# The opening transfers of a one-core hybrid encoder step: reordered, cut finer, spread over two queues

## The chip, the core and the metric

The kernel runs on one core of a Trainium2 chip. The metric is the device time of one execution in microseconds (us), median of several runs. The engines are named as in the profile: PE is TensorE (matrix products; PEld its weight loads), DVE is VectorE, ACT is ScalarE, POOL is GpSimd, SP is SyncE, which issues most transfers.

## What is computed

One inference step of a two-layer encoder over 288 rows (256 of a prompt, 32 of a running stream) of width 2048, in float32. Layer 0 mixes tokens by a gated MLP, layer 1 by retention; each is followed by a SwiGLU feed-forward part and each residual by a layer norm:

```
x = layer_norm(ALPHA * x + mixer(x), ...)
x = layer_norm(ALPHA * x + swiglu(x, w_ffn_in[i], w_ffn_out[i]), ...)
# the first mixer begins with the product that this change feeds:
z = gelu(x @ w_in)              # w_in: 2048 x 4096
u, v = split(z, 2);  v = layer_norm(v)
```

## The kernel before, in words

All weights lie in one packed array, cut into chunks of 512 KB: 128 partitions by eight blocks of 128x128. The blocks are packed in the order in which PE uses them. Float32 products are made of two halves: `split` (L591) casts a raw chunk on ACT to its high part (`whi`, L592) and subtracts on DVE to get the low part (`wlo`, L593). The same is done with each tile of x (`xh`, `xl`; loaded raw into `y`). For each block, `step` (L106) issues three products in this order: high by high (L112), high weights by low x (L113), low weights by high x (L114). PE runs in the order of the program; `prep` (L69) is called when a chunk's first block comes up and prepares three chunks ahead.

The first product group (`core.group("a_in", ...)`, L728) takes eight column tiles at once, so that chunk c, for c from 0 to 15, holds the eight blocks that meet x tile c. A chunk of the group therefore needs the x tile of its number too. Raw chunks go through a ring of three buffers (`raw`), the halves through rings of four (`whi`, `wlo`). SP's queue issues the transfers in the order of the program's schedule; a transfer into a ring buffer waits until the DVE subtraction that last read it is done. ACT, DVE and SP run their own instructions strictly in the order given.

At the start (L1114 to L1130) ACT loads its table, PE runs eleven warming products of a constant tile (L1117), and chunks 0 to 3 and x tiles 0 to 3 are prepared by hand order on ACT and DVE. Chunk 0 comes in two halves, chunk 1 whole, x in pairs of tiles. Further x tiles follow by `load` (L1120) from the group's hook, and after some steps `tables` (L627) brings the mask and mixing weights that DVE multiplies (`g_ws`, L633) and ACT casts (`g_w`, L638).

Of the kernel before, what the change touches and what calls it, by code (L numbers as in the profile page):

```python
# [10 lines left out]
F32 = mybir.dt.float32  # L11
# [8 lines left out]
P = 128  # L20
D = 2048
KT = D // P
NP = 256
NS = 32
NT = NP + NS
NH = NT // 2
ROW = 320
# [11 lines left out]
CB = 8  # L39
# [11 lines left out]
class Core:  # L51


    def __init__(self, ctx, tc, wpack):
        self.tc, self.nc, self.wpack = tc, tc.nc, wpack
        self.order = []
        self.wp = ctx.enter_context(tc.tile_pool(name="wp", bufs=4))
        self.wp.tile([P, 16], F32, tag="shift", name="shift_wp", bufs=1)
        self.acc = ctx.enter_context(tc.tile_pool(name="acc", bufs=4, space=PSUM))
        self.aux = ctx.enter_context(tc.tile_pool(name="aux", bufs=4, space=PSUM))  # L60
        self.dram = ctx.enter_context(tc.tile_pool(name="dram", bufs=1, space=bass.MemoryType.DRAM))
        self.ready = {}
        self.keep = {}
        self.nprep = 0
        self.todo = []
        self.soon = []
        self.ticks = 0

    def prep(self, upto, between=None):  # L69
        nc = self.nc  # L70
        while self.nprep <= upto and self.nprep < NCH:
            c = self.nprep
            raw = self.wp.tile([P, CB * P], F32, tag="raw", name=f"raw{c}", bufs=3)
            hi = self.keep[c] if c in self.keep else self.wp.tile([P, CB * P], F32R, tag="whi", name=f"whi{c}")
            lo = self.wp.tile([P, CB * P], F32R, tag="wlo", name=f"wlo{c}")
            n = CB * P
            dma, cut = {0: (n // 2, n // 4), 1: (n, n // 2)}.get(c, (n, n))
            for o in range(0, n, cut):
                if o % dma == 0:
                    nc.sync.dma_start(raw[:, o:o + dma], self.wpack[c][:, o:o + dma])  # L80
                q = slice(o, o + cut)
                split(nc, hi[:, q], lo[:, q], raw[:, q])
                if between is not None and o == 0:
                    between()
            self.ready[c] = (hi, lo)
            self.nprep += 1

# [497 lines left out]
def moving(pool, n, name, tag=None, lead=False):  # L585

    t = pool.tile([P, n, ROW], F32R, name=name, **({"tag": tag} if tag else {}))
    return t if lead else t[:, :, LEAD:]


def split(nc, hi, lo, f, pin=lambda i: i):  # L591
    pin(nc.scalar.copy(hi, f))  # L592
    nc.vector.tensor_tensor(lo, f, hi.bitcast(F32), ALU.subtract)  # L593


def to_rows(nc, room, src, w, prompt, sample):


    blocks = room.rearrange("(b s) f -> s b f", s=32)
    for a in range(4):  # L600
        nc.gpsimd.dma_start(blocks[:, :, a * w:(a + 1) * w], src[32 * a:32 * a + 32, :, :])
    nc.gpsimd.dma_start(prompt, room[:NP, :].rearrange("(t p) f -> p t f", p=P))
    nc.gpsimd.dma_start(sample, room[NP:, :])


def gmlp(core, cst, x, y, lnp, ins, v_out, load):
    tc, nc = core.tc, core.nc
    xh, xl = x
    xs = lambda k: (xh[:, k, :NT], xl[:, k, :NT])
    with ExitStack() as es:  # L610
        pool = es.enter_context(tc.tile_pool(name="gm", bufs=1, reuse_waits="tile"))
        sh = moving(pool, KT, "g_sh")
        tv = pool.tile([P, KT * ROW], F32, tag="sl", name="g_tv")
        tv = tv[:, :KT * NT].rearrange("p (q b i s) -> p q b i s", q=4, b=9, i=4)
        vp = pool.tile([P, 2, D], F32, name="g_vp")
        vs = y.rearrange("p k n -> p (k n)")[:NS, :D]
        v3 = pool.tile([NR, D], F32R, name="g_v3")
# [17 lines left out]
        def sample_weights():  # L635
# [2 lines left out]
                nc.scalar.copy(w3[r * NS:(r + 1) * NS], w)  # L638
            nc.vector.tensor_tensor(w3[2 * NS:], w, w3[:NS].bitcast(F32), ALU.subtract)

        nc.gpsimd.memset(nrm[:, 2, 0:2], 1.0)
        core.after(6, tables)
        core.after(12, sample_weights)
# [2 lines left out]
        def v_evac(m, ps):  # L646
            j = m - 16
            vg = pool.tile([P, NT], F32, tag="u", name=f"vg{j}", bufs=8)
            nc.scalar.activation(vg, ps[:, :NT], AF.Gelu)
            q, i = divmod(j, 4)  # L650
            nc.vector.transpose(tv[:, q, :, i, :], vg)
            if i == 3:
                t = tv[:, q, :, :, :].rearrange("p b i s -> p b (i s)")
                cs = slice(q * 512, (q + 1) * 512)
                to_rows(nc, core.room([NT, 512], f"g_room{q}"), t, P, vp[:, :, cs], vs[:NS, cs])
                core.after(2, lambda: v_rows(q))

        def v_rows(q):
            for t in range(3):
                n = rows[t]  # L660
                tc.keep_in_program_order(nc.vector.bn_stats(st[:n, t, q, :], vt[t][:n, q * 512:(q + 1) * 512]))
            if q == 3:
                v_stats()
# [62 lines left out]
        late = {}  # L726
        gbs = {}
        core.group("a_in", 0, list(range(KT)), list(range(16, 24)), xs, v_evac, load, lag=0)  # L728
        core.tiles("a_in", 0, list(range(KT)), list(range(24, 32)), xs, v_evac, grouped=False)
        core.tiles("a_in", 0, list(range(KT)), list(range(16)), xs, u_evac, grouped=False)  # L730
        ln = PostNorm(core, cst, x, y, lnp, 0)
# [361 lines left out]
@with_exitstack  # L1093
def hybrid_step(ctx, tc, ins, outs):
    nc = tc.nc
    ctx.enter_context(tc.manual_schedule(engines={PE}))
    core = Core(ctx, tc, ins["wpack"])
    cp = ctx.enter_context(tc.tile_pool(name="cp", bufs=1))
    lnp = ctx.enter_context(tc.tile_pool(name="lnp", bufs=1))
    cp.tile([P, 72], F32, name="shift")  # L1100
    lnp.tile([P, 32], F32, name="shift_lnp")
    core.wide_x = moving(cp, KT, "xh", lead=True)
    xh = core.wide_x[:, :, LEAD:]
    core.wide_l = moving(cp, KT, "xl", lead=True)
    xl = core.wide_l[:, :, LEAD:]
    y = cp.tile([P, KT, NT], F32, name="y")
    cst = {}
    cp.tile([P, 40], F32, name="shift_one")
    cst["one2048"] = cp.tile([P, P], F32, name="one2048")
    nc.gpsimd.memset(cst["one2048"], 1.0 / D)  # L1110
    cst["ln"] = cp.tile([P, 4, 2, KT], F32, name="lnv")
    cst["one_r"] = cp.tile([P, P], F32R, name="one_r")
    cp.tile([P, 56], F32, name="shift_end")
    core.tables("gelu_and_others")  # L1114
    nc.scalar.copy(cst["one_r"], cst["one2048"])
    warm = core.bank("warm")
    for _ in range(11):  # L1117
        nc.tensor.matmul(warm[:, :P], cst["one2048"], cst["one2048"], start=True, stop=True)

    def load(k):  # L1120
        if k < KT:
            if k % 2 == 0:
                nc.sync.dma_start(y[:, k:k + 2, :], ins["xT"][:, k:k + 2, :])
            split(nc, xh[:, k, :NT], xl[:, k, :NT], y[:, k, :])

    with tc.manual_schedule(engines={mybir.EngineType.DVE, mybir.EngineType.Activation}):
        core.prep(0, lambda: load(0))
        for k in range(1, 4):
            load(k)
            core.prep(k)  # L1130
    x = (xh, xl)
    ln = gmlp(core, cst, x, y, lnp, ins, outs["v"], lambda s: load(s + 4))
    ln = ffn(core, cst, x, y, lnp, 0, ln)
    ln = retention(core, cst, x, y, lnp, ln, ins, outs["st_p"], outs["st_s"])
    ffn(core, cst, x, y, lnp, 1, ln, outs["yT"], ins["gb_rows"])
    core.flush()
    assert len(core.order) == NBLK + NSTATE
    return core.order
# [85 lines left out]
```

## Time and profile before

| | |
|---|---|
| time, median of 3 runs | 2770.11 us (2769.72 to 2770.37) |
| the profiled execution's own time | 2770.98 us |
| its span, first to last instruction | 2769.2 us |
| PE busy | 2762.4 us |
| DVE busy | 1699.9 us |
| ACT busy | 1258.9 us |
| moved by DMA | 515.53 MB, mean 186 GB/s |

The page gives busy times of the engines, a strip of the span in 40 slices, and the chain of work that ended last. The first slice is 69 us long, so what this change touches has to be read from narrower views: rows of the timeline (start, duration, engine, line, operation, output from inputs, and in brackets the idle time before it with what ended it), and windows (for each engine busy time and a count of instructions; then the granted PE clock, the busy share of the DMA engines and GB/s).

### The profile page before, as it was taken

How to read it: one execution, taken by the hardware profiler on the slowest of the kernel's cores; microseconds unless marked ns; L12 is line 12 of the kernel's file. 1: busy time of each engine (PE TensorE's matmuls, PEld its weight loads, DVE VectorE, ACT ScalarE, POOL GpSimd, SP SyncE). 2: the span in 40 equal slices, each digit the busy share in tenths (PEclk: the TensorE clock that was granted, in tenths of full speed). 3: DMA queues.
4: the chain of work that ended last, by engine and by line, in shares of the span. 5: the costliest groups of instructions: out<-in, count | busy, mean ns of one | idle time of the engine just before them, and what ended most of it. 6: DMA issues, size and time to landing. Idle time of an engine off the chain costs nothing.

```text
span 2769.2 us, 51638 instructions
## 1 busy us (share of the span) xinstructions
PE 2762.4 (100%) x21618; PEld 2752.1 (99%) x21618; DVE 1699.9 (61%) x2493; ACT 1258.9 (45%) x1701; POOL 144.7 (5%) x245
## 2 busy tenths in 40 slices
PE   9999999999999999999999999999999999999999
PEld 9999999999999999999999999999999999999999
DVE  6688964445444456877765666767854445444466
ACT  5455554433344344644543444455643433444444
POOL 1100000000000000012200111210000000000001
PEclk9999999999999999999999999999999999999999
DMA  8655555555555555567765666765555555555554
GB/s 278 213 188 168 168 175 175 173 172 173 176 174 172 173 176 182 169 213 233 238 204 176 195 218 213 224 207 173 171 172 175 175 172 173 174 175 173 172 174 141
DMA packets 146794, 515.53 MB, mean 186 GB/s; under 512 B 18096, under 2 KB 20800, under 8 KB 146528
## 3 DMA queue, kind: packets, MB, share of 16 engines
q1 hardware_dynamic: 132272, 473.62, 51.6%
q0 software_dynamic: 14288, 38.60, 4.7%
q8 instruction: 169, 2.77, 0.4%
q14 instruction: 65, 0.53, 0.1%
HBM read 486.99 MB, written 25.17 MB: 185 GB/s over the span
## 4 chain that ended last, share of the span: by engine, by line
PE 98%; DMA 1%; DVE 1%; issue 0%; POOL 0%; ACT 0%; SPq 0%; POOLq 0%; DVEq 0%; ACTq 0%
PE af_in L112 13%; PE af_in L114 13%; PE af_in L113 13%; PE ab_in L112 7%; PE ab_in L114 7%; PE ab_in L113 7%; PE af_out L113 6%; PE af_out L112 6%; PE af_out L114 6%; PE ab_out L114 2%; PE ab_out L112 2%; PE ab_out L113 2%; PE aa_in L114 2%; PE aa_in L113 2%; PE aa_in L112 2%; PE aa_out L112 1%
## 5 line engine op out<-in xcount | busy, mean ns | idle before, releaser
L593 DVE TENSOR_TENSOR wlo<-raw,whi 128x1024 fp32r<-128x1024 f32 (+1 forms) x885 | 1076.8, 1218 | 839.7 <-ACT whi L592 835.9
L592 ACT CAST whi<-raw 128x1024 fp32r<-128x1024 f32 (+1 forms) x885 | 927.5, 1049 | 1306.1 <-PE af_in L113 328.9
L112 PE MATMUL af_in<-xh,whi 128*128 128x288 f32 (+1 forms) x2816 | 814.1, 289 | 0.0
L114 PE MATMUL af_in<-xh,wlo 128*128 128x288 f32 (+1 forms) x2816 | 813.8, 289 | 0.0
L113 PE MATMUL af_in<-xl,whi 128*128 128x288 f32 x2816 | 812.8, 289 | 0.0
L113 PEld LDWEIGHTS af_in<-xl,whi 128*128 128x128 f32 x2816 | 528.6, 188 | 0.0
L114 PEld LDWEIGHTS af_in<-xh,wlo 128*128 128x128 f32 x2816 | 528.6, 188 | 0.0
L112 PEld LDWEIGHTS af_in<-xh,whi 128*128 128x128 f32 x2816 | 528.4, 188 | 0.0
L112 PE MATMUL ab_in<-xh,whi 128*128 128x288 f32 (+1 forms) x1536 | 444.9, 290 | 0.0
L114 PE MATMUL ab_in<-xh,wlo 128*128 128x288 f32 (+1 forms) x1536 | 444.2, 289 | 0.0
L113 PE MATMUL ab_in<-xl,whi 128*128 128x288 f32 x1536 | 443.6, 289 | 0.0
L113 PE MATMUL af_out<-hl,whi 128*128 128x288 f32 x1320 | 380.5, 288 | 0.0
L113 PEld LDWEIGHTS ab_in<-xl,whi 128*128 128x128 f32 x1536 | 288.4, 188 | 0.6
L112 PEld LDWEIGHTS ab_in<-xh,whi 128*128 128x128 f32 x1536 | 288.3, 188 | 0.5
L114 PEld LDWEIGHTS ab_in<-xh,wlo 128*128 128x128 f32 x1536 | 288.3, 188 | 0.0
L113 PEld LDWEIGHTS af_out<-hl,whi 128*128 128x128 f32 x1320 | 247.5, 188 | 0.0
L114 PE MATMUL af_out<-hh,wlo 128*128 128x288 f32 x704 | 203.2, 289 | 0.0
L112 PE MATMUL af_out<-hh,whi 128*128 128x288 f32 x704 | 203.2, 289 | 0.0
L112 PE MATMUL af_out<-hid,whi 128*128 128x288 f32 x616 | 177.3, 288 | 0.0
L114 PE MATMUL af_out<-hid,wlo 128*128 128x288 f32 x616 | 177.3, 288 | 0.0
L112 PE MATMUL aa_in<-xh,whi 128*128 128x288 f32 x512 | 148.1, 289 | 0.3 <-ACT xh L592 0.3
L114 PE MATMUL aa_in<-xh,wlo 128*128 128x288 f32 x512 | 147.5, 288 | 0.7 <-DVE wlo L593 0.7
(293 smaller groups left out, 3555.9 us busy)
## 6 DMA issues: line engine op xcount, KB each, us to landing
raw<-in_wpack_dram SPq DMA_DIRECT2D x887, 512.0 KB, 3.3
v_room<-tv POOLq DMA_DIRECT2D x32, 144.0 KB, 4.6
of<-o_room POOLq DMA_DIRECT2D x32, 144.0 KB, 5.5
vw<-v_room POOLq DMA_DIRECT2D x8, 512.0 KB, 6.7
out_st_s_dram<-sso POOLq DMA_DIRECT2D x16, 256.0 KB, 2.6
out_st_p_dram<-so POOLq DMA_DIRECT2D x16, 256.0 KB, 5.0
o_room<-to POOLq DMA_DIRECT2D x8, 512.0 KB, 3.9
y<-in_xT_dram SPq DMA_DIRECT2D x8, 288.0 KB, 5.7
```

The lines of the kernel that those rows point to most:

```text
L112: mm(wide, hi, halves(xh, lead), start=first, stop=False)
L113: mm(halves(ps[:, lead:], 0, lead), hi, halves(xl), start=False, stop=False)
L114: mm(wide, lo, halves(xh, lead), start=False, stop=last)
L592: pin(nc.scalar.copy(hi, f))
L593: nc.vector.tensor_tensor(lo, f, hi.bitcast(F32), ALU.subtract)
```

## The change

Nine warming products stand in place of eleven. The first transfers are written out in a new function `begin`, called inside the first mixer, in the order in which they are used: x tile 0 alone, chunk 0 in a quarter, a quarter and a half, x tile 1 alone, chunk 1 in two halves, x tiles 2 and 3, chunk 3, x tiles 4 and 5, chunk 4, all in SP's queue. Chunk 2 is issued from ACT's queue, after the cast of x tile 0. Chunks 3 and 4 get buffers of their own: they are put in the space that later holds the mixer's tile `g_tv`, which is now allocated at its first use. The cast and subtraction of x tile 0 come ahead of those of chunk 0.

```diff
+    def send(self, c, ends, queue):
+        raw = self.spare[c] = self.raw(c)
+        self.sent.add(c)
+        o = 0
+        for e in ends:
+            queue.dma_start(raw[:, o:e], self.wpack[c][:, o:e])
+            o = e
...
-            dma, cut = {0: (n // 2, n // 4), 1: (n, n // 2)}.get(c, (n, n))
+            if c not in self.sent:
+                nc.sync.dma_start(raw, self.wpack[c])
+            cut = {0: n // 4, 1: n // 2}.get(c, n)
...
-        tv = pool.tile([P, KT * ROW], F32, tag="sl", name="g_tv")
+        raw = pool.tile([P, KT * ROW], F32, tag="sl", name="g_raw")
+        core.spare = {c: raw[:, (c - 3) * CB * P:(c - 2) * CB * P] for c in (3, 4)}
...
-    for _ in range(11):
+    for _ in range(9):
...
+    def begin():
+        n = CB * P
+        fetch(0, 1)
+        core.send(0, (n // 4, n // 2, n), nc.sync)
+        fetch(1, 1)
+        core.send(1, (n // 2, n), nc.sync)
+        fetch(2, 2)
+        core.send(3, (n,), nc.sync)
+        fetch(4, 2)
+        core.send(4, (n,), nc.sync)
+        with tc.manual_schedule(engines={mybir.EngineType.DVE, mybir.EngineType.Activation}):
+            for k in range(4):
+                load(k)
+                if k == 0:
+                    core.send(2, (n,), nc.scalar)
+                core.prep(k)
```

SP's queue at the start of the program before (`y` is x's raw tiles, 288 columns each; `raw` a chunk of 1024 columns or a part of it):

```order
L80 DMA raw_102<-in_wpack_dram 128x512
L1123 DMA y<-in_xT_dram 128x576
L80 DMA raw_102<-in_wpack_dram 128x512
L80 DMA raw_120<-in_wpack_dram 128x1024
L1123 DMA y<-in_xT_dram 128x576
L80 DMA raw_131<-in_wpack_dram 128x1024
L80 DMA raw_139<-in_wpack_dram 128x1024
```

and the same place now:

```order
L1137 DMA y<-in_xT_dram 128x288
L79 DMA raw_113<-in_wpack_dram 128x256 x2
L79 DMA raw_113<-in_wpack_dram 128x512
L1137 DMA y<-in_xT_dram 128x288
L79 DMA raw_118<-in_wpack_dram 128x512 x2
L1137 DMA y<-in_xT_dram 128x576
L79 DMA g_raw<-in_wpack_dram 128x1024
L1137 DMA y<-in_xT_dram 128x576
L79 DMA g_raw<-in_wpack_dram 128x1024
```

Chunk 2 (`raw_131` before) is gone from this queue, and chunks 3 and 4 need no buffer to come free. ACT at the start now, where `raw_129` is chunk 2:

```order
L603 CAST xh<-y 128x288
L79 DMA raw_129<-in_wpack_dram 128x1024
L603 CAST whi_131<-raw_113 128x256 x4
L603 CAST xh<-y 128x288
L603 CAST whi_143<-raw_118 128x512 x2
L603 CAST xh<-y 128x288
L603 CAST whi_151<-raw_129 128x1024
```

The cast of x tile 0 moved ahead of chunk 0's, and behind it stands the new issue. The order of the casts of x tiles 1 and 2 against chunks 1 and 2 is as it was.

Further on, ACT's casts of chunks 11 to 14 with the mixing weights between them, before (`whi_424` is chunk 11):

```order
L592 CAST whi_424<-raw_423 128x1024
L592 CAST whi_457<-raw_456 128x1024
L638 CAST g_w_153<-g_ws 32x1024
L592 CAST whi_489<-raw_488 128x1024
L638 CAST g_w_153<-g_ws 32x1024
```

and now (`whi_423` is chunk 11):

```order
L603 CAST whi_423<-raw_422 128x1024
L649 CAST g_w_105<-g_ws 32x1024
L603 CAST whi_456<-raw_455 128x1024
L649 CAST g_w_105<-g_ws 32x1024
```

The first cast of the mixing weights now stands ahead of chunk 12, where it stood ahead of chunk 13. PE's order is the same but for the two warming products.

More of the change, by code (lines that the diff above doesn't have):

```diff
@@ L63, in __init__ @@
         self.keep = {}
+        self.spare = {}
+        self.sent = set()
         self.nprep = 0
@@ L67, in __init__, with raw, prep @@
         self.ticks = 0
-    def prep(self, upto, between=None):
+    def raw(self, c):
+        return self.spare.pop(c) if c in self.spare else self.wp.tile([P, CB * P], F32, tag="raw", name=f"raw{c}", bufs=3)
+    def send(self, c, ends, queue):
[5 more added lines that the diff above has]
+            o = e
+    def prep(self, upto):
         nc = self.nc
@@ L72, in prep @@
             c = self.nprep
-            raw = self.wp.tile([P, CB * P], F32, tag="raw", name=f"raw{c}", bufs=3)
+            raw = self.raw(c)
             hi = self.keep[c] if c in self.keep else self.wp.tile([P, CB * P], F32R, tag="whi", name=f"whi{c}")
@@ L76, in prep @@
             n = CB * P
-            dma, cut = {0: (n // 2, n // 4), 1: (n, n // 2)}.get(c, (n, n))
+            if c not in self.sent:
+                nc.sync.dma_start(raw, self.wpack[c])
+            cut = {0: n // 4, 1: n // 2}.get(c, n)
             for o in range(0, n, cut):
-                if o % dma == 0:
-                    nc.sync.dma_start(raw[:, o:o + dma], self.wpack[c][:, o:o + dma])
                 q = slice(o, o + cut)
                 split(nc, hi[:, q], lo[:, q], raw[:, q])
-                if between is not None and o == 0:
-                    between()
             self.ready[c] = (hi, lo)
@@ L603, in to_rows, with gmlp @@
     nc.gpsimd.dma_start(sample, room[NP:, :])
-def gmlp(core, cst, x, y, lnp, ins, v_out, load):
+def gmlp(core, cst, x, y, lnp, ins, v_out, begin, load):
     tc, nc = core.tc, core.nc
@@ L612, in gmlp @@
         sh = moving(pool, KT, "g_sh")
-        tv = pool.tile([P, KT * ROW], F32, tag="sl", name="g_tv")
-        tv = tv[:, :KT * NT].rearrange("p (q b i s) -> p q b i s", q=4, b=9, i=4)
+        raw = pool.tile([P, KT * ROW], F32, tag="sl", name="g_raw")
+        core.spare = {c: raw[:, (c - 3) * CB * P:(c - 2) * CB * P] for c in (3, 4)}
         vp = pool.tile([P, 2, D], F32, name="g_vp")
@@ L639, in sample_weights @@
             nc.vector.tensor_tensor(w3[2 * NS:], w, w3[:NS].bitcast(F32), ALU.subtract)
+        begin()
         nc.gpsimd.memset(nrm[:, 2, 0:2], 1.0)
@@ L650, in v_evac @@
             q, i = divmod(j, 4)
+            if j == 0:
+                t = pool.tile([P, KT * ROW], F32, tag="sl", name="g_tv")
+                late["tv"] = t[:, :KT * NT].rearrange("p (q b i s) -> p q b i s", q=4, b=9, i=4)
+            tv = late["tv"]
             nc.vector.transpose(tv[:, q, :, i, :], vg)
@@ L1116, in hybrid_step, with fetch @@
     warm = core.bank("warm")
-    for _ in range(11):
+    for _ in range(9):
         nc.tensor.matmul(warm[:, :P], cst["one2048"], cst["one2048"], start=True, stop=True)
+    def fetch(k, n):
+        nc.sync.dma_start(y[:, k:k + n, :], ins["xT"][:, k:k + n, :])
     def load(k):
         if k < KT:
-            if k % 2 == 0:
-                nc.sync.dma_start(y[:, k:k + 2, :], ins["xT"][:, k:k + 2, :])
+            if k % 2 == 0 and k > 4:
+                fetch(k, 2)
             split(nc, xh[:, k, :NT], xl[:, k, :NT], y[:, k, :])
[L1126 to L1130, printed above, removed]
+    def begin():
[14 more added lines that the diff above has]
+                core.prep(k)
     x = (xh, xl)
-    ln = gmlp(core, cst, x, y, lnp, ins, outs["v"], lambda s: load(s + 4))
+    ln = gmlp(core, cst, x, y, lnp, ins, outs["v"], begin, lambda s: load(s + 4))
     ln = ffn(core, cst, x, y, lnp, 0, ln)
```

## The prediction

> **What bounds the kernel now.** The page comes first: busy times, then the chain of work that ended last.
>
> ```profile
> span 2769.2 us, 51638 instructions
> PE 2762.4 (100%) x21618; PEld 2752.1 (99%) x21618; DVE 1699.9 (61%) x2493; ACT 1258.9 (45%) x1701; POOL 144.7 (5%) x245
> PE 98%; DMA 1%; DVE 1%; issue 0%; POOL 0%; ACT 0%; SPq 0%; POOLq 0%; DVEq 0%; ACTq 0%
> ```
>
> PE is busy for all but 6.8 us of the span, and the chain is PE's for 98%. PE's own work does not change apart from two warming products, so only its start and its holes can be worth anything. The second view is the list of waits, for PE between 6.3 and 2760 us:
>
> ```profile
> PE aa_in L114 <- DVE wlo L593: 0.7, 1, 0.7
> ```
>
> There is one hole, 0.7 us long, at about 134 us, in front of a product that waits for a low part. The rest of the question is the start. The chain of the first 40 us begins with:
>
> ```profile
> 0.75 0.39 SPq L80
> 1.20 3.94 DMA y<-in_xT_dram
> 5.17 0.44 ACT xh L592
> 5.63 0.47 DVE xl L593
> 6.14 0.40 PE aa_in L113
> ```
>
> The first x pair, issued second, lands 3.94 us after its issue; its cast and subtraction follow, and PE starts. The timeline shows PE there (start, duration):
>
> ```profile
> 4.37 1.00 PE L1118 MATMUL warm<-one 128*128 128x128 f32 x7
> 5.65 0.40 PE L112 MATMUL aa_in<-xh,whi 128*128 128x288 f32 x1 [0.28 <-ACT xh L592]
> 6.14 0.40 PE L113 MATMUL aa_in<-xl,whi 128*128 128x288 f32 x1
> 9.17 0.29 PE L112 MATMUL aa_in<-xh,whi 128*128 128x288 f32 x1
> 12.21 0.29 PE L112 MATMUL aa_in<-xh,whi 128*128 128x288 f32 x1
> 12.46 0.29 PE L114 MATMUL aa_in<-xh,wlo 128*128 128x288 f32 x1
> ```
>
> Chunk 1 starts at 9.17 and chunk 2 at 12.21: a chunk takes PE 3.04 us when nothing stops it. Counted back from 12.21, chunk 0 would have had to start at 6.13 to be in step. **6.13 is the number that the change can move**, as every later product follows in step from it.
>
> **The change part by part.** *Nine warming products.* A warming product is two records (22 for 11). The seven last of them start at 4.37 and later; their durations (least, median, largest, in ns) and the last start are in the row of line 1118 for 4.5 to 6 us:
>
> ```profile
> L1118 PE MATMUL warm<-one x8: 274/275/421, 4.2 to 5.1; 128*128 128x128 f32 x8
> ```
>
> From 4.37 to 5.1 there are six steps, 0.12 us each. With four records fewer PE is free for its next product at 5.1 + 0.12 - 4 x 0.12 = 4.74. If everything else were there, PE would be in step from then, a gain of 6.13 - 4.74 = **1.39 us**. That is the most that this change can bring at the start.
>
> *The first operands.* Three transfers of the trace give the delay from issue to landing, least, median and largest: the first half of chunk 0 (issued at 0.75), the first x pair (1.20) and chunk 2 (3.09).
>
> ```profile
> DMA to landing us min/median/max: 2.6/2.6/2.6
> DMA to landing us min/median/max: 3.9/3.9/3.9
> DMA to landing us min/median/max: 6.7/6.7/6.7
> 3.39 0.40 ACT L592 CAST whi<-raw 128x256 fp32r<-128x256 f32 x1 [1.05 <-DMA raw<-in_wpack_dram]
> ```
>
> x tile 0, now first and smaller than that first half, should land by 0.75 + 2.6 = 3.35. Its cast takes 0.43 (below), its subtraction 0.47: both parts by 4.3. Behind the cast ACT issues chunk 2, which costs ACT between nothing and the 0.43 us that SP takes for an issue; then the first quarter's cast, 0.40. That is 4.2 to 4.6, before PE is free. So the issue on ACT is hidden, by warming products, with 0.2 us to spare; without that cover it would cost up to 0.43.
>
> *Chunk 2 and x tile 2, the part that decides.* By chunk 2 PE has caught up with the transfers. The windows (busy time and count of PE, PEld, DVE, ACT, POOL; PE clock; share of the DMA engines; GB/s):
>
> ```profile
> 1.50:2.00 0.50, 0.50 (x4) 0.50 (x4) 0.00 (x0) 0.50 (x1) 0.00 (x0) 1.00 0.30 53
> 2.00:2.50 0.50, 0.50 (x5) 0.50 (x4) 0.00 (x0) 0.33 (x2) 0.00 (x0) 1.00 0.87 311
> 2.50:3.00 0.50, 0.50 (x4) 0.50 (x4) 0.00 (x0) 0.00 (x0) 0.00 (x0) 1.00 0.94 247
> 0.00:8.50 8.50, 7.12 (x41) 6.72 (x42) 2.43 (x7) 4.51 (x10) 0.96 (x7) 1.00 0.75 254
> 8.50:9.00 0.50, 0.50 (x6) 0.50 (x5) 0.50 (x1) 0.50 (x2) 0.00 (x0) 1.00 0.46 139
> 4.00:6.00 2.00, 1.72 (x11) 1.36 (x10) 0.62 (x2) 0.74 (x2) 0.00 (x0) 1.00 1.00 344
> 6.00:8.00 2.00, 1.91 (x15) 1.86 (x15) 1.55 (x5) 1.29 (x4) 0.00 (x0) 1.00 0.97 385
> ```
>
> 8.5 us at 254 GB/s are 2.16 MB, which is x tiles 0 to 3 and chunks 0 to 2 (4 x 0.147 MB and 3 x 0.524 MB). The engines are about full from 2 us on, so these bytes can't come faster in another order; only a hole behind them, at 8.5 to 9.0, is filled by the buffers of chunks 3 and 4. Chunk 2 counted as landed at 3.09 + 6.7 = 9.8, some 1.25 us behind its last bytes. The first half of chunk 0 (0.262 MB) was moved by 2.8 us (0.182 MB by 2.5, the rest at 247 GB/s) and landed at 3.35, 0.55 behind. So the last of the same 2.16 MB lands at L between 8.5 + 0.55 = 9.05 and 9.8. Now it is x tiles 2 and 3, because chunk 2 comes in beside them. I take the middle, **L = 9.4**. What follows a landing:
>
> ```profile
> 8.81 0.43 ACT L592 CAST xh<-y 128x288 fp32r<-128x288 f32 x1
> 9.77 1.05 ACT L592 CAST whi<-raw 128x1024 fp32r<-128x1024 f32 x1 [0.53 <-DMA raw<-in_wpack_dram]
> 10.86 1.23 DVE L593 TENSOR_TENSOR wlo<-raw,whi 128x1024 fp32r<-128x1024 f32 x1 [0.78 <-ACT whi L592]
> 10.73 0.42 ACT L592 CAST xh<-y 128x288 fp32r<-128x288 f32 x1
> 11.07 1.05 ACT L592 CAST whi<-raw 128x1024 fp32r<-128x1024 f32 x1
> ```
>
> From the cast of chunk 2 to the end of its subtraction: 12.09 - 9.77 = 2.32. The cast of an x tile ahead of it takes ACT 0.34 (10.73 to 11.07). The low part is there at L + 2.66, and the third product of chunk 2, 0.25 behind its first, waits for it; the chunk then is in step from L + 2.41 = 11.81, against 12.21. Before, the low part was there at 12.09 for a product at 12.46. So the new order spends the 0.37 us of slack and puts an x cast in front. **Gain 0.40 us**, 0.75 with L = 9.05, 0.01 with 9.8.
>
> *Chunk 1* gives the same. Ahead of its first half's end stand 1.08 MB in SP's queue and, if the other queue goes first, chunk 2's 0.52: by the windows' rates 1.6 MB are in by 6.85, landed by 7.4 to 8.1.
>
> ```profile
> 7.76 1.14 ACT L592 CAST whi<-raw 128x512 fp32r<-128x512 f32 x2 [0.48 <-DMA raw<-in_wpack_dram]
> 8.42 1.29 DVE L593 TENSOR_TENSOR wlo<-raw,whi 128x512 fp32r<-128x512 f32 x2 [0.61 <-ACT whi L592]
> ```
>
> Half a chunk's low part comes 1.3 us after its cast begins (7.76 to 9.07), here at 8.7 to 9.4, so chunk 1 is in step from 8.45 to 9.15 against 9.17.
>
> [...]
>
> *Finer transfers.* Rows of 1 KB and 1.2 KB do not occur at the start of this trace. Taken as fast as the rows of 2 KB, which ran at about 290 GB/s, they cost nothing; at half that rate the first 410 KB would be 1.4 us later, and L 10.8. I take nothing, and keep 10.8 as an outer end.
>
> *The later hole* at 134 us hangs on a chain that itself starts from PE at 106 us and runs in the same order, so it moves along whole: 0.
>
> **Sum.** The profiled execution took 2770.98 us, 1.8 more than its span; with 0.40 less it would be 2770.6. The runs shown have a median of 2770.11, so **2769.7**.
>
> **The rivals.** *The whole gain* (A): chunks 1 and 2 come in time because PE waits for nothing but the warming products: 1.39 less, 2768.7. For it: the hole at 8.5; against it: the full DMA engines. That takes L = 4.74 + 6.08 - 2.41 = 8.4, earlier than the bytes.
>
> *No gain or a small loss* (B): the last landing stays 1.25 us behind its bytes, or small rows are dearer, and the x cast in front of chunk 2 eats the rest. L from 9.8 to 10.8 gives between 0 and 1.0 us lost: 2770.1 to 2771.1. The wait on the second x tile pair then takes the place of the wait on the first.
>
> *A new wait at chunk 12* (C), which ends slower. The mixing weights now stand before chunk 12 on ACT and DVE, where they stood before chunk 13.
>
> ```profile
> 30.12 0.33 SPq L80 DMA_DIRECT2D raw<-in_wpack_dram  x1
> 31.63 0.83 SPq L80 DMA_DIRECT2D raw<-in_wpack_dram  x1
> 32.50 0.43 SPq L629 DMA_DIRECT2D g_mask<-in_mask_dram  x1
> 38.41 0.90 DVE L633 TENSOR_TENSOR g_ws<-g_ws,g_mask 128x128 f32<-128x128 f32 x4 [2.25 <-DMA g_mask<-in_mask_dram]
> 43.61 1.22 DVE L593 TENSOR_TENSOR wlo<-raw,whi 128x1024 fp32r<-128x1024 f32 x1
> ```
>
> DVE waits for the mask until 38.41 and chunk 13's low part, queued behind, is done at 44.83; its product is due at 12.46 + 11 x 3.04 = 45.9. Chunk 12's is due at 45.9 - 3.04 - 0.40 = 42.5. The mask is issued behind chunk 12's transfer now, not chunk 13's, 1.5 us earlier by those rows (30.12 against 31.63): low part at 43.3, a stall of 0.8, net 0.4 slower, 2770.5. With the mask no earlier at all the stall is 2.3 and the time 2772.0. It decides from a mask later than 36.1 us. Against it: two more buffers let the early casts run ahead, and the mask's 5.9 us in the queue should shrink with the backlog.
>
> **How the numbers follow.** Forecast (gain 0.1 to 0.75): 0.50. B: 0.22. A: 0.11. C: 0.13. Something unforeseen: 0.04. A measurement here can tell about 0.2%, 5.5 us, from no change; none of the cases reaches that, so "same" holds 0.97, faster 0.01, slower 0.02 for the unforeseen. The range runs from A's 2768.7 to 2771.1, the outer end of B, which takes in the small stall of C.
>
> **What would show it.** Right: first product at 4.8 to 5.1 us; chunk 1 and chunk 2 each waiting once, PE in step from about 5.7 counted back; the x pair behind chunk 1 landing at 9.0 to 9.8; no hole near 42 us; the hole at 134 us unchanged in size. Wrong: no waits in chunks 1 and 2 (A); PE in step only from 6.1 or later (B); DVE idle for the mask and a PE hole near 42 us (C); a first product well after 5.1, which would mean that small first transfers land no sooner.

## The result and the profile after

The changed kernel takes **2773.77 us** (median of 22 runs, 2770.68 to 2778.45), the kernel before 2770.1 us beside it (22 runs, 2769.37 to 2772.31). The ratio is 1.0012, with an interval of 1.0007 to 1.0018. That is 3.7 us slower, less than the 0.2% (5.5 us) that the prediction counts as no change, but the interval leaves 1 out, and outside the range of 2768.7 to 2771.1. The runs also spread over 8 us where those of before spread over 3.

The profiled execution took 2772.8 us, 1.8 more than that of before, so it shows about half of the loss. First its page:

```profile
span 2770.9 us, 51635 instructions
PE 2763.2 (100%) x21614; PEld 2752.9 (99%) x21614; DVE 1699.6 (61%) x2493; ACT 1259.3 (45%) x1701; POOL 144.7 (5%) x245
PE 98%; DMA 1%; DVE 1%; issue 0%; SPq 0%; POOL 0%; ACT 0%; POOLq 0%; ACTq 0%
```

The page tells nothing: PE is still all of the chain. The waits of PE from 4.5 us on do:

```profile
PE aa_in L123 <- ACT whi L603: 1.6, 1, 1.6
PE aa_in L125 <- DVE wlo L604: 0.5, 2, 0.3
```

A wait of 1.6 us on a high part is new. The one on low parts is two now: 0.2 at the start and 0.3 at the old place near 136 us, where before had 0.7. Where the new wait stands is in PE's timeline (start, duration):

```profile
4.87 0.59 PE L123 MATMUL aa_in<-xh,whi 128*128 128x288 f32 x1
10.79 0.40 PE L123 MATMUL aa_in<-xh,whi 128*128 128x288 f32 x1 [1.55 <-ACT whi L603]
11.52 0.40 PE L125 MATMUL aa_in<-xh,wlo 128*128 128x288 f32 x1 [0.20 <-DVE wlo L604]
14.42 0.29 PE L123 MATMUL aa_in<-xh,whi 128*128 128x288 f32 x1
```

PE starts chunk 0 at 4.87, 0.78 earlier than before. Then it waits for chunk 1, which starts at 10.79 where before started it at 9.17, and waits again within it. In front of chunk 2 it waits for nothing. Chunk 2 starts at 14.42; counted back by two chunks of 3.04, PE is in step from 8.34, and before it was from 6.13: 2.2 us lost at the start, 0.4 given back at 136 us, 1.8 in all. The chain of the first 40 us names the transfer:

```profile
3.09 7.01 DMA raw<-in_wpack_dram
10.12 0.63 ACT whi L603
10.77 0.70 DVE wlo L604
11.52 0.40 PE aa_in L125
```

The first half of chunk 1, issued at 3.09, lands 7.01 us later. ACT's timeline shows what lands late and what does not:

```profile
3.07 0.43 ACT L603 CAST xh<-y 128x288 fp32r<-128x288 f32 x1 [0.73 <-DMA y<-in_xT_dram]
3.08 0.38 ACTq L79 DMA_DIRECT2D raw<-in_wpack_dram  x1
4.27 0.76 ACT L603 CAST whi<-raw 128x256 fp32r<-128x256 f32 x2 [0.77 <-DMA raw<-in_wpack_dram]
8.16 0.43 ACT L603 CAST xh<-y 128x288 fp32r<-128x288 f32 x1 [1.71 <-DMA y<-in_xT_dram]
10.12 1.18 ACT L603 CAST whi<-raw 128x512 fp32r<-128x512 f32 x2 [1.53 <-DMA raw<-in_wpack_dram]
```

x tile 0 is there at 3.07. x tile 1 comes at 8.16 and chunk 1 at 10.12, both issued about when ACT issued chunk 2 (3.08). Chunk 2 itself landed 6.8 us after that issue, at 9.9, ahead of the first half of the chunk that is due before it. And the bytes are fewer; the same window that gave 254 GB/s in before, and two more that are needed below:

```profile
0.00:8.50 8.50, 7.50 (x38) 7.50 (x39) 2.00 (x5) 3.83 (x8) 0.96 (x7) 1.00 0.71 214
6.00:8.00 2.00, 2.00 (x13) 2.00 (x13) 0.76 (x2) 0.46 (x2) 0.00 (x0) 1.00 1.02 320
0.00:10.10 10.10, 8.23 (x42) 8.01 (x42) 2.46 (x6) 3.92 (x8) 0.96 (x7) 1.00 0.76 240
```

214 GB/s over 8.5 us are 1.82 MB, where before had moved 2.16.

### The profile page after: what moved, and what is told of

Same layout as the page of the kernel before. It is cut to its first block, busy times and chain, and to the rows that moved or that the text cites. A ratio compares the mean times of both kernels' runs of the same rounds, so it can differ in the third digit from the quotient of the medians.

```text
span 2770.9 us, 51635 instructions
## 1 busy us (share of the span) xinstructions
PE 2763.2 (100%) x21614; PEld 2752.9 (99%) x21614; DVE 1699.6 (61%) x2493; ACT 1259.3 (45%) x1701; POOL 144.7 (5%) x245
## 4 chain that ended last, share of the span: by engine, by line
PE 98%; DMA 1%; DVE 1%; issue 0%; SPq 0%; POOL 0%; ACT 0%; POOLq 0%; ACTq 0%
PE af_in L125 13%; PE af_in L123 13%; PE af_in L124 13%; PE ab_in L123 7%; PE ab_in L125 7%; PE ab_in L124 7%; PE af_out L124 6%; PE af_out L125 6%; PE af_out L123 6%; PE ab_out L123 2%; PE ab_out L125 2%; PE ab_out L124 2%; PE aa_in L125 2%; PE aa_in L123 2%; PE aa_in L124 2%; PE aa_out L123 1%
```

## The experiments

Two theories came from that profile. **S**: chunk 2 in the second queue delays what SP's queue needs first. **F**: the finer pieces at the head cost it. The number of warming products (**G**) and the two extra buffers (**B**, not the prediction's rival of that letter) were the other suspects. A further theory, **T**, came out of the profiles. Medians in us, with before's from the same series (runs of a kernel before beside them) and the ratio's interval:

| run, edit | median (range) | before | ratio |
|---|---|---|---|
| e1: chunk 2 in SP's queue | 2771.05 (2770.46-2773.38) | 2770.04 | 1.0001 [0.9992, 1.0010] |
| e2: coarser pieces | 2773.36 (2771.85-2775.41) | 2770.04 | 1.0010 [1.0002, 1.0019] |
| e3: without the two buffers | 2773.83 (2770.87-2776.08) | 2770.04 | 1.0013 [1.0004, 1.0022] |
| e4: eleven warming products | 2773.54 (2770.22-2776.49) | 2770.04 | 1.0011 [1.0003, 1.0020] |
| e6: e1 and e2 together | 2770.75 (2769.74-2772.87) | 2769.82 | 1.0005 [0.9996, 1.0013] |
| e7: products in the wait, in ten groups | 2787.58 (2787.20-2789.39) | 2769.82 | 1.0066 [1.0053, 1.0078] |
| e8: before with the two buffers | 2770.37 (2769.18-2772.53) | 2769.82 | 1.0001 [0.9992, 1.0009] |
| e9: chunk 2 from ACT 2.5 us later | 2776.84 (2775.46-2778.86) | 2769.82 | 1.0026 [1.0015, 1.0036] |
| e10: in effect the change again | 2773.47 (2770.75-2776.05) | 2770.14 | 1.0009 [1.0000, 1.0019] |
| e11: in effect e6 again | 2770.74 (2770.08-2772.55) | 2770.14 | 1.0001 [0.9992, 1.0010] |
| e5: before with nine warming products | 2770.22 (2769.28-2774.62) | 2770.14 | 1.0002 [0.9993, 1.0011] |
| e12: products in the wait, first group only | 2772.11 (2771.32-2774.06) | 2769.70 | 1.0008 [0.9999, 1.0016] |
| e13: e6 with four such products | 2770.82 (2770.07-2772.80) | 2769.70 | 1.0002 [0.9993, 1.0011] |

(The ranges of e10 and e11 leave out one execution each, of 12,944 and 4,008 us; the medians count it.)

**e1, one queue.** The edit:

```diff
         fetch(2, 2)
+        core.send(2, (n,), nc.sync)
         core.send(3, (n,), nc.sync)
...
-                if k == 0:
-                    core.send(2, (n,), nc.scalar)
```

> The changed kernel with chunk 2 taken out of ACT's queue and put into SP's, behind x tiles 2 and 3. Theory S (the second queue is the cause: chunk 2 is served beside x tile 1 and chunk 1 and holds them up): x tile 1 and chunk 1's first half land some 1 to 2 us sooner (the half by about 8.3 us instead of 10.1), PE's wait of 1.6 us at chunk 1 shrinks to under 0.5, and the time falls from 2773.8 to 2771 to 2772. Theory F (the finer transfers are the cause: rows of 1 KB are slow): the half still lands after 9.3 and the time stays at 2773 or more. Theory B (chunks 3 and 4, now queued early behind, slow everything): likewise no change.

Measured: 2771.05, 2.7 us under the change. ACT's timeline of e1:

```profile
6.88 0.62 ACT L603 CAST whi<-raw 128x512 fp32r<-128x512 f32 x1 [0.44 <-DMA raw<-in_wpack_dram]
9.31 0.62 ACT L603 CAST whi<-raw 128x512 fp32r<-128x512 f32 x1 [1.80 <-DMA raw<-in_wpack_dram]
11.35 1.05 ACT L603 CAST whi<-raw 128x1024 fp32r<-128x1024 f32 x1 [0.84 <-DMA raw<-in_wpack_dram]
```

The first half of chunk 1, issued at 3.09 as in the change, is there at 6.88 and not at 10.12; the price is chunk 2, cast at 11.35. Its bytes are no faster (211 GB/s over the first 8.5 us): **the second queue changed what came first, not how much came.** S holds for most of the loss, and some 1.0 us over before are left. What makes the bytes fewer is open: over the same window the profiles of before, e5 and e8 moved 254 to 267 GB/s, those of e6, e11 and e13 227 to 250, and those of the change and the forms that issue alike (e4, e7, e10, e12) 210 to 240.

**e2, e3, e4: the other parts, one at a time.** The edits to the change are

```diff
-        core.send(0, (n // 4, n // 2, n), nc.sync)
+        core.send(0, (n // 2, n), nc.sync)
...
-        core.send(1, (n // 2, n), nc.sync)
+        core.send(1, (n,), nc.sync)
```

for e2; for e3 the lines that give chunks 3 and 4 buffers and transfers of their own are left out; for e4 `range(9)` is `range(11)`.

> The changed kernel with chunk 0 sent in two halves and chunk 1 whole, as before the change; chunk 2 stays in ACT's queue, x tiles 0 and 1 stay single. Theory F: by 8.5 us the queues have moved 2.1 MB again instead of 1.8, and the time falls by 1 us or more, to 2772.8 or less. Theory S: within 0.7 us of the changed kernel, 2773 to 2774.5, with PE still waiting over 1 us at chunk 1 (a little longer, since chunk 1 now counts as landed only whole).

> The changed kernel without the two more raw buffers: chunks 3 and 4 come through the ring, as before, so nothing but x tiles 4 and 5 is queued behind x tiles 2 and 3 early on. Theory B: landings come closer behind their bytes, chunk 1's first half by 9 us, the time 2772 or less. Theories S and F: no change at the start, PE's wait at chunk 1 stays at 1.3 us or more, time 2773 to 2775.

> The changed kernel with eleven warming products again. In the changed kernel's trace PE went at half pace until 7.1 us (a product each 0.24 us), where the kernel before changed pace at about 4.5. Theory G (two warming products fewer let the clock open late, and that costs): the pace changes by about 5 us and the time falls by 0.7 us or more. Theories S and F: PE waits for chunk 1 anyway, so an earlier or faster chunk 0 only waits longer: time within 0.5 us of the changed kernel, 2773.3 to 2774.3.

All three stay within 0.41 us of the change. F, B and G alone carry none of the loss that can be told while the second queue stands; the single intervals are some 2.5 us to either side.

**e6, e8, e5: the same parts without the second queue.** e6 joins the edits of e1 and e2; e8 is before with only the two extra buffers; e5 is before with nine warming products.

> Chunk 2 in SP's queue as in the first experiment, and in addition chunk 0 in two halves and chunk 1 whole. With one queue the changed kernel still took 1.0 us more than the kernel before (2771.05 against 2770.04). Theory F (what is left is the finer transfers): 2770.1 or less, chunk 2 landing before 9.8 us. Theory O (what is left is the order: with chunk 2 last or x tile 2 late, the slack at chunk 2 is spent whatever the sizes): 2770.7 to 2771.5, PE waiting in chunk 2.

> The kernel before with one part of the change alone: chunks 3 and 4 have buffers of their own, and so are sent without waiting for the ring; order, sizes, queue and eleven warming products as before. Theory H (the hole in the transfers at 8.5 to 9 us is worth filling): 2769.7 or less. Theory N (chunk 3 has 1.5 us of slack anyway): 2769.9 to 2770.3, no change. Theory B again (a longer queue behind makes landings late): 2770.5 or more.

> The kernel before with nine warming products instead of eleven, nothing else. In its profile the first chunk's data end the wait and not the warming products (first product at 5.65, warming products done at 5.3), so both theories give no change: 2769.8 to 2770.5, ratio within 0.9997 to 1.0005. Rival (fewer warming products let the full clock come later or be lost again): 0.5 to 1.5 us slower, 2770.4 to 2771.5.

e5 is 0.1 above its before, e8 0.6, both with 1 well inside the interval: neither part does anything that can be told. e6 is 0.9 above its before and 0.6 in its repeat (e11). The time is what theory O gave, but PE waits at chunk 1 and not, as O had it, in chunk 2. e6's issue of chunk 1, the delay to its landing, ACT's cast of it, and PE's two waits:

```profile
2.62 0.43 SPq L79 DMA_DIRECT2D raw<-in_wpack_dram  x1
DMA to landing us min/median/max: 5.8/5.8/5.8
8.45 1.14 ACT L603 CAST whi<-raw 128x512 fp32r<-128x512 f32 x2 [0.99 <-DMA raw<-in_wpack_dram]
9.12 0.39 PE L123 MATMUL aa_in<-xh,whi 128*128 128x288 f32 x1 [0.33 <-ACT whi L603]
9.84 0.40 PE L125 MATMUL aa_in<-xh,wlo 128*128 128x288 f32 x1 [0.21 <-DVE wlo L604]
```

Before issued chunk 1 at 2.14, it landed 5.6 later and was cast at 7.76. e6 has one more transfer ahead of it (x tiles 0 and 1 apart), which puts its issue 0.48 later. Chunk 2 shows the same: issued at 3.09 in before, 3.56 in e6 and, behind three more transfers, 4.51 in e1, it landed 6.7, 6.9 and 6.8 later. So each further cut put a later transfer off by about one issue of SP, 0.47 us. In e6 PE is in step from 6.67 (before 6.13), 0.54 later, which has about the size of one issue; this rests on profiles alone, no run took it apart.

**e9, the second queue later.** Chunk 2 is issued by ACT behind chunk 0's casts:

```diff
-                if k == 0:
-                    core.send(2, (n,), nc.scalar)
                 core.prep(k)
+                if k == 0:
+                    core.send(2, (n,), nc.scalar)
```

> The changed kernel with chunk 2 still issued from ACT's queue, but behind the casts of chunk 0 instead of behind the first cast of x: about 3 us later, at 6 us instead of 3.1. Theory S as sharing of the engines (what matters is that x tile 1 and chunk 1 are served first): chunk 1's first half lands by 8 us, time 2771 to 2772, as with one queue. If the second queue itself is the harm, wherever it starts: 2773 or more.

Measured: 2776.84, 3.1 us slower than the change. ACT's timeline of e9:

```profile
5.57 0.38 ACTq L79 DMA_DIRECT2D raw<-in_wpack_dram  x1
7.36 1.26 ACT L603 CAST whi<-raw 128x512 fp32r<-128x512 f32 x2 [0.16 <-DMA raw<-in_wpack_dram]
13.80 1.04 ACT L603 CAST whi<-raw 128x1024 fp32r<-128x1024 f32 x1 [3.58 <-DMA raw<-in_wpack_dram]
```

Chunk 1 is there at 7.36, as S wants, but S's time (2771 to 2772) was missed: now chunk 2 takes 8.2 us to land, beside the chunks 3 and 4 that SP issued at 4.51 and 5.56. So S holds for which transfer is put off, and at neither of the two moments tried did the second queue help: at 3.1 us chunk 1 came late, at 5.6 us chunk 2 did.

**T, the clock.** Windows of 3.41 us, in e3 (busy time and count of PE, PEld, DVE, ACT, POOL; granted PE clock; DMA share; GB/s):

```profile
core 0: us, PE busy (x) PEld busy (x) DVE busy (x) ACT busy (x) POOL busy (x), PEclk, DMA share, GB/s
9.06:12.47 3.41, 1.12 (x6) 0.90 (x7) 1.35 (x3) 1.95 (x4) 0.00 (x0) 1.00 0.86 343
12.47:15.88 3.41, 3.41 (x17) 3.41 (x16) 3.12 (x7) 3.26 (x8) 0.00 (x0) 0.50 0.66 205
15.88:19.30 3.42, 3.42 (x29) 3.42 (x29) 2.54 (x3) 1.96 (x3) 0.00 (x0) 1.00 0.84 286
```

After PE's wait at chunk 1 (here 2.6 us) the granted clock is 0.50 from 12.47 to 15.88, and PE gets through 17 products where it gets through 29 in the next window: 12 x 0.127 = 1.5 us lost behind a wait that is over. From its first product to that of chunk 2, chunk 1 takes 5.24 us in e3 (11.14 to 16.38) and 3.63 in the change. The change's own profile has no such stretch:

```profile
3.73:7.15 3.42, 3.42 (x16) 3.42 (x16) 1.80 (x5) 1.48 (x4) 0.00 (x0) 1.00 0.95 298
7.15:10.56 3.41, 2.09 (x16) 1.86 (x15) 0.46 (x1) 0.87 (x2) 0.00 (x0) 1.00 0.99 348
10.56:13.97 3.41, 2.98 (x21) 2.75 (x22) 2.81 (x5) 3.31 (x6) 0.00 (x0) 1.00 1.01 405
```

(The first row prints 1.00 ahead of the first clock record, but 16 products in 3.42 us are the half pace; the full clock came at 7.15 here, at 4.48 in before, at 5.64 in e3.) Its wait straddles two windows and leaves 3.41 - 2.09 = 1.32 us idle in the one and 0.43 in the other. The windows are counted from the moment the full clock came and are as long as the stretch at 0.50 in e3, 3.41 us. The ones with most idle time, each with the window behind it, in e4, e2 and e9:

```profile
7.60:11.01 3.41, 1.54 (x10) 1.09 (x9) 1.32 (x3) 1.67 (x4) 0.00 (x0) 1.00 1.04 413
11.01:14.42 3.41, 3.41 (x17) 3.41 (x16) 3.09 (x5) 3.33 (x6) 0.00 (x0) 0.50 1.03 408
```

```profile
8.81:12.23 3.42, 1.36 (x8) 1.14 (x9) 1.59 (x3) 2.24 (x4) 0.00 (x0) 1.00 1.03 417
12.23:15.64 3.41, 3.41 (x17) 3.41 (x16) 3.26 (x6) 3.09 (x6) 0.00 (x0) 0.50 1.03 398
```

```profile
9.98:13.40 3.42, 2.03 (x16) 1.80 (x15) 0.46 (x1) 0.25 (x1) 0.00 (x0) 1.00 1.02 412
13.40:16.81 3.41, 1.17 (x7) 0.95 (x8) 1.93 (x3) 3.00 (x6) 0.00 (x0) 1.00 0.79 314
16.81:20.22 3.41, 3.41 (x17) 3.41 (x16) 3.41 (x5) 2.55 (x4) 0.00 (x0) 0.50 0.71 243
```

In the profiles with such windows (before, the change, e2, e3, e4, e9, e10, e12), those with 1.39 us idle or less are followed by the full clock, and those with 1.87 us or more (e4 1.87, e2 2.06, e9 2.24, e3 2.29) by one window at half clock. (The expectation of e12 counts from start to start and has 2.19 and 1.55 for the same bounds.) The moment of the full clock differs between executions in which PE issues the same products up to the end of chunk 0, the first at 4.87 us in each: about 5.8 us in e7, 6.57 in e9, 7.15 in the change, 7.16 in e10. A wait of some 2 us cost 1.5 us more in one execution and nothing more in another: e4's 1.7 us had the stretch behind it, the 2.0 us of e10, which is in effect the change again, had not. No profile of the change itself caught the stretch.

The waits with such a stretch behind them lasted from 1.7 us (e4, whose row follows) to 2.9 us (e9), and most of each fell into one window.

```profile
PE aa_in L123 <- ACT whi L603: 1.7, 1, 1.7
```

The test fills the wait with products that nothing needs. e7 was the first form:

```diff
             if hook is not None:
+                if s == 0:
+                    for _ in range(8):
+                        self.nc.tensor.matmul(ps[ms[0]][:, 320:448], self.one, self.one, start=False, stop=False)
                 hook(s)
...
+    core.one = cst["one2048"]
```

> The changed kernel with eight more products of the constant tile put into PE's order between chunk 0 and chunk 1, accumulated into columns 320 to 447 of a bank that nothing reads; so PE has 1.7 us more work at full pace, all of it where it waits. Theory T (the wait of about 2 us lets the clock gate drop to half pace for one stretch of 3.4 us, and chunk 2 then takes 5.2 us instead of 3.04): no drop, chunk 2 takes under 3.7 us in the profile, and the time falls by 1 us or more, to 2772.7 or less, although PE has more to do. Without T (the loss is the wait alone): the products cost nothing or up to 1 us, 2773.5 to 2774.8.

It came out 14 us slower, for a reason outside the theory. The products of its line:

```profile
L177 PE MATMUL af_in<-one x96: 272/275/275, 307.7 to 2013.4; 128*128 128x128 f32 x96
L177 PE MATMUL ab_in<-one x48: 273/275/275, 1117.3 to 1166.4; 128*128 128x128 f32 x48
L177 PE MATMUL aa_in<-one x16: 272/275/275, 8.5 to 10.1; 128*128 128x128 f32 x16
```

They were issued in ten groups, not one. 144 of the 160 records stand in later groups, where PE has no wait; at 0.107 us a record they cost 15.4 us. That leaves 2772.2, under the change by 1.6, but as an estimate. e10 and e11 were to issue them in the first group only, with a condition `w == "aa_in" and s == 0`. The group is called by another name than its tile, so no such product was issued:

> The changed kernel with eight products of the constant tile between chunk 0 and chunk 1 of the first group only (16 records of 107 ns at full clock, 1.71 us, into columns that nothing reads; they add work and leave out none). In the earlier form they also stood ahead of nine later groups, 144 records or 15.4 us, which leaves some 2772.2 of its 2787.58. Theory T (a TensorE that waits 2 to 3 us at chunk 1 is granted half the clock for 3.413 us once more, and this makes the changed kernel's long runs): the products keep it busy there, so the median falls to 2771.3 to 2772.4 and the longest run stays under 2774. Rival (late landings alone make the time; the half-clock stretch comes whether TensorE waits or works): the products are only extra work beside the wait, median 2773.5 to 2775, runs spread over 2771 to 2778 as before.

> One queue for all early transfers (chunk 2 behind x tiles 2 and 3 on SP), chunk 0 in halves, chunk 1 whole, nine warming products, two more raw buffers, and four products of the constant tile (8 records, 0.86 us) between chunk 0 and chunk 1. Without the four it took 2770.75, with 0.62 us of wait before chunk 1 and 0.49 within it in its profile. Theory T with S (second queue): nothing is left but the landings; the four take the place of the wait, 2770.2 to 2770.9, and no run over 2772.5. Rival (the half-clock stretch plays no part where one queue is used): 0.2 to 0.9 us slower than without, 2771 to 2771.7.

They test nothing of T; they repeat the change (2773.47 after 2773.77) and e6 (2770.74 after 2770.75). e12 and e13 issue the products in the first group, once:

```diff
+                if self.fill and s == 0:
+                    self.fill = False
+                    for _ in range(8):
+                        self.nc.tensor.matmul(ps[ms[0]][:, 320:448], self.one, self.one, start=False, stop=False)
...
+    core.one = cst["one2048"]
+    core.fill = True
```

(four in e13).

> The changed kernel with eight products of the constant tile (16 records of 107 ns, 1.71 us) between chunk 0 and chunk 1 of the first group, this time issued once and only there. Theory T, made sharper by the profiles so far: half the clock comes for 3.413 us when TensorE was idle for over some 2 us of the 3.413 us before (2.19 to 2.45 us in the four profiles with such a stretch, 1.55 at most in the nine without). The products cut the idle time at chunk 1 from 1.8-2.9 us to under 1.2, so the stretch goes: profile without it, median 2771.3 to 2772.6, longest run under 2775. Rival (late landings alone make the time): the products hide in the wait or add to it, median 2773.3 to 2774.5 and runs up to 2776 or more.

> One queue for all early transfers, chunk 0 in halves, chunk 1 whole, with four products of the constant tile (8 records, 0.86 us) between chunk 0 and chunk 1. Without them 2770.75 and 2770.74 in two series, TensorE idle for at most 0.72 us of any 3.413 us stretch in their profiles. Theory T: there is no half-clock stretch to take away, and the four lie in a wait of 0.6 to 0.8 us: no change, 2770.5 to 2771.1. Rival (waits of this size also bring a half-clock stretch in many runs): 2770.0 to 2770.4.

Measured: e12 2772.11, longest run 2774.06; e13 2770.82. Both are as T said. In e12's windows:

```profile
5.83:9.25 3.42, 3.42 (x30) 3.42 (x29) 1.13 (x3) 0.84 (x3) 0.00 (x0) 1.00 0.99 308
9.25:12.66 3.41, 3.04 (x23) 2.62 (x22) 1.69 (x4) 2.63 (x5) 0.00 (x0) 1.00 1.02 408
12.66:16.07 3.41, 3.41 (x29) 3.41 (x28) 3.41 (x6) 3.11 (x6) 0.00 (x0) 1.00 1.03 400
```

PE is idle for 0.37 us of the window of the wait, and the clock stays at 1.00. **Work added in a wait made the kernel faster**, by 1.7 us against the change's 2773.77 and by 1.4 against its repeat's 2773.47, with the transfers about as late: chunk 1's cast begins at 9.90 in e12's profile. Counted from the before of each series, which differ a little, the gain is 1.3 and 0.9 us (2.4 over before, against 3.7 and 3.3). The ratios' intervals overlap (0.9999 to 1.0016 and 1.0007 to 1.0018), so the size is known roughly; that the half-clock stretch is a cost of its own is what the windows of e2, e3, e4 and e9 show.

Every execution also lists its mean granted clock, from which a stretch of 3.41 us at 0.50 takes 0.0006. It is 0.999 in 18 of the change's 22 executions and 1.000 in 4; in e12 it is 0.999 in 4 of 11, and in the 33 of before beside e1 in 10. That fits T but is a hint only: the profiles of before and e12 list 0.999 too, without the stretch.

No version tried beats the kernel before.

## Why the prediction was wrong, point by point

- *The first operands, nine warming products.* Right: x tile 0 at 3.07 (3.35 said), first product at 4.87 (4.8 to 5.1 said). It is worth nothing that can be told, as e5 shows the same for the warming products alone. The gain "in step from 4.74" took full pace from the first product on; at half pace until 7.15, chunk 0's products end at 9.08, in step from 6.04 only. The wait for chunk 1 hid this.
- *Chunk 1, "gives the same".* **This is the step that failed.** The sum let chunk 2 go ahead and charged its bytes alone: 1.6 MB in by 6.85, landed 0.55 to 1.25 behind, at 7.4 to 8.1, and nothing lost at chunk 1 (in step from 8.45 to 9.15 against 9.17). The half landed at 10.10, and chunk 1 starts at 10.79. By the windows 1.6 MB were in only at 7.75, 0.9 late, and the landing was 2.35 behind that; by 10.10 the engines had moved 2.42 MB, 0.8 more than the sum counted ahead of it. With one queue (e1) the half landed at 6.86, 0.9 behind its 1.08 MB (in by 6.0), as the sum's distance has it. The half's cast begins at 6.88 with one queue and at 10.12 with two. The difference, 3.2 us, is twice what chunk 2's 0.52 MB cost at the 320 GB/s of 6 to 8 us (1.6 us); what took the rest no run shows.
- *"The engines are about full from 2 us on, so these bytes can't come faster in another order."* They came slower, 1.82 MB by 8.5 us and not 2.16, and with two queues in another order than that of use: chunk 2 at 9.9, the first half of chunk 1 at 10.10. A busy share near 1.00 was read as a fixed rate; from 6 to 8 us the share was 1.02 at 320 GB/s, where before had 0.97 at 385.
- *L, the last of x tiles 2 and 3, "the part that decides".* 9.4 said, 9.0 to 9.8 as bounds, 10.8 as an outer end for dear small rows. Issued at 4.04, they landed after

```profile
DMA to landing us min/median/max: 7.3/7.3/7.3
```

that is at 11.3. But it decided nothing: by the prediction's own sum L = 11.3 allows chunk 2 in step at 11.3 + 2.41 = 13.7, and the wait at chunk 1 had already put it at 14.42. PE was to be in step from 5.73 and is from 8.34.
- *The clock.* The sum priced a wait at its length. In the profiles of e2, e3, e4 and e9 the wait at the start cost some 1.5 us more than it lasted. By e12, T adds some 0.9 to 1.7 us to the median of the change; for the change itself this is inferred, as its own profile has no such stretch.
- *Finer transfers, extra buffers: 0.* The buffers: right (e3, e8). The finer pieces: no difference that can be told beside the second queue (e2), 0.3 between e1 and e6, less than one issue of SP (0.47 us).
- *"The later hole ... moves along whole: 0".* Wrong in a small way. It was 0.7 in before's profile and e1's, 0.3 in the change's, and in e2, e5 and e8 PE waits nowhere after 14 us. It does not follow the parts of the change, so it should have stood in the sum with a bound on either side.
- *The rivals.* B had the right sign, but the wrong place and too small a price: it had PE wait on the second x tile pair, in front of chunk 2, and PE waits at chunk 1. A and C did not happen: PE waits for nothing near 42 us. The range ended with B's 1.0 us at 2771.1; the one larger loss reckoned, C's 2772.0, was left outside it and was for another place.

The parts, by medians: one queue instead of two takes 2.7 of the 3.7 us off (2773.77 to 2771.05). T is 0.9 to 1.7 of these by e12: with one queue the longest wait of PE at the start was 0.7 us (e1; 0.3 in e6, none in e13) and no half-clock stretch was seen, so the two overlap and are not to be added. The last 0.6 to 1.1 (e1, e6, e11, e13) lie within what the single intervals leave open.

## What to carry to other kernels

Here one queue already kept the DMA engines at a busy share of 0.90 from 2 to 6.5 us (e1), and a second one added no rate (0.88 in the change; over the first 8.5 us 211 GB/s with one, 214 with two); it let a transfer that was due later come in ahead of the one due next (chunk 2 at 9.9, the first half of chunk 1 at 10.10). Before spreading transfers, ask which landing is due next and what would then arrive beside it. Waits of PE of 1.7 to 2.9 us soon after its start had 3.41 us at half clock behind them in four profiles (e2, e3, e4, e9), which cost some 1.5 us each; 1.6 us in the change and 2.0 us in e10 had none. Look for a stretch at 0.50 in windows behind the wait, and judge such changes by many runs.

## What the runs showed that was not expected

The same program ran its first group at two paces. e6 and e11 issue the same products in the same order. PE in the stretch from 60 to 120 us, in e6 and then in e11:

```profile
60.00:120.00 60.00, 60.00 (x476) 60.00 (x475) 32.13 (x37) 23.86 (x30) 11.53 (x19) 1.00 0.77 249
```

```profile
60.00:120.00 60.00, 60.00 (x468) 60.00 (x467) 32.91 (x37) 23.11 (x29) 11.89 (x20) 1.00 0.75 242
```

476 products against 468, with no wait and the clock at 1.00 in both: 1.7% slower. Each 30 us from 30 to 120 us hold 235 products in e11 and 239 or 240 in e6; from 140 to 200 us both have 480. Over some 130 us that is 2.2 us, as an estimate. The profiled execution of e11 took 2772.41 against 2770.51. From 60 to 120 us e1 (467) and e9 (468) show the slower pace too, before (475) and the change (476) the faster one. It may be why the runs of one kernel fall into two groups about 2 us apart (e11: six from 2770.1 to 2770.7, four from 2772.2 to 2772.6); no run here tells what sets it.
